# w_down by seven half-size products per quarter of the inner features, token-major

## Chip, core and metric

The kernel runs on one core of one Trainium2 chip. The metric is the device time of one execution in microseconds (us). A core has five engines that run their own instruction streams in order and wait for each other by semaphores: TensorE (PE; its weight loads are listed as PEld), VectorE (DVE), ScalarE (ACT), GpSimd (POOL) and SyncE (SP), which issues the DMAs here.

## Reference

One layer of a decoder on 512 tokens of width 1024: a token mixer (gated linear attention beside block-sparse attention), a squared-ReLU MLP, and a gated per-layer embedding, all in float32. The change lies in the MLP; what stands around it:

```python
y = jax.nn.sigmoid(gate_a) * y_a + jax.nn.sigmoid(gate_b) * y_b
x = x + y @ w_out[i]

h2 = rms_norm(x, norm_mlp[i])
x = x + jnp.square(jax.nn.relu(h2 @ w_up[i])) @ w_down[i]      # 1024 -> 4096 -> 1024

ple_gate = jax.nn.sigmoid(rms_norm(x, norm_ple[i]) @ w_ple_gate[i])
x = x + ple_gate * (p[i] @ w_ple[i])
```

## The kernel before

**Arithmetic.** Every large product is made of three matmuls (`mm3`, L99 to 103): both operands are split into a high half, rounded to the matmul's type, and a low half, the rest; high x high, high x low and low x high are added up in one PSUM bank. Splitting takes one ScalarE copy for the high half and one subtraction for the low half, on VectorE unless GpSimd is named (`split` L89, `halves` L150).

**Weights.** All weights come through one list, `stream` (L219 to 238), in units of 128 x 1024 elements (512 KB). `fetch` (L142) loads the next unit into one of three `raw` buffers by a DMA on SP's queue; `convert` (L168) pops the oldest raw, makes its high and low halves `whi` and `wlo` (three buffers each), puts the pair into `ready`, and fetches another. A unit's 24 matmuls use a pair from `ready`.

**Order of the work.** The schedule is by hand: program order is each engine's order. `gemm_fm` (L180) makes one 128-feature tile of a feature-major result (features in partitions, 512 tokens in columns): the weights are the stationary operand, and each unit is two halves of 12 matmuls, with a `tick` after each. `gemm_tm` (L196) makes a token-major result: activations are stationary and weights move. `tick` (L113) runs every job that is due for one step; jobs are generators started by `spawn` (L108), `yield 1` lets a job go on at the next tick, and `yield 0` later in the same tick. Small work of the other engines is so placed between halves of units. Results go to PSUM, two banks `acc` and six banks `aux`, and an evacuation (`evac`) reads them.

**The MLP (L747 to 790).** For each of two halves of the 4096 inner features: 16 tiles of w_up, each evacuated by VectorE (`up_evac` L754: ReLU and the norm's factor R1), squared by ScalarE (L765) and split into `ff` high and low; then 8 tiles of w_down with two units each (`nu=2`), added by VectorE to the residual stream `x1` (`down_evac` L769). x1 is feature-major and lies in SBUF slots c0 and c1. After the second half each tile is also scaled and split for the next product (`scaled_split` L94), its square is added up (`add_square` L303), and after the last tile `norm_end` (L293) is started: it splits the sum of squares at one tick, makes its mean over features on TensorE at the next (`mean_sq` L275), and then R2.

**The end.** `gemm_ple` (L795) makes four tiles of w_ple in 24 matmuls, `gemm_fm` eight tiles of w_gate, and the rest of w_ple follows.

Of the kernel before, what the change touches and what calls it, by code (L numbers as in the profile page):

```python
# [27 lines left out]
P = 128  # L28
# [18 lines left out]
def kernel(ctx: ExitStack, tc: tile.TileContext, xT, pT, w_in, w_val, w_glr, w2, cols,  # L47
# [5 lines left out]
    tmp = ctx.enter_context(tc.tile_pool(name="tmp", bufs=2))  # L53
    accp = ctx.enter_context(tc.tile_pool(name="acc", bufs=2, space=PSUM))
    auxp = ctx.enter_context(tc.tile_pool(name="aux", bufs=6, space=PSUM))
    ctx.enter_context(tc.manual_schedule())

    uid = [0]
# [49 lines left out]
    def spawn(gen, wait=0):  # L108


        jobs.append([gen, wait])

    def tick():  # L113
        due = []
        for j in list(jobs):
            if j[1] > 0:
                j[1] -= 1
            else:
                due.append(j)
        while due:  # L120
            again = []
            for j in due:
                try:
                    n = next(j[0])
                except StopIteration:
                    jobs.remove(j)
                    continue
                if n:
                    j[1] = n - 1
                else:  # L130
                    again.append(j)
            due = again
# [84 lines left out]
    def kt_of(hi, lo):  # L217
        return lambda k: (hi[:, k], lo[:, k])
# [514 lines left out]
    h2_lo = slot("a5", [P, KT, T], F32R)  # L733
    R1 = const.tile([P, T], F32, tag="R", name="R1")
    s1 = tt("s")

    def out_evac(i, ps):
# [9 lines left out]
    h3_hi = h3_lo = s2 = R2 = None  # L747
    for half in range(2):
        ff = [slot(t, [P, KT, T], F32R) for t in ("a0", "a1", "a2", "a6")]

        def ff_of(k, ff=ff):
            return ff[2 * (k // 8)][:, k % 8], ff[2 * (k // 8) + 1][:, k % 8]

        def up_evac(i, ps, half=half, ff_of=ff_of):  # L754
            e = tt("e")
            if half or i:
                V.scalar_tensor_tensor(e, ps, 0.0, R1, ALU.max, ALU.mult)  # L757
            else:
                A.activation(e, ps, AF.Relu)

            def rest():
                if not half and not i:
                    yield 2
                    V.tensor_tensor(e, e, R1, ALU.mult)
                A.activation(e, e, AF.Square)  # L765
                split(*ff_of(i), e)
            spawn(rest())

        def down_evac(i, ps, half=half):  # L769
            nonlocal h3_hi, h3_lo, s2, R2  # L770
            V.tensor_tensor(x1[i], ps, x1[i], ALU.add)  # L771
            if not half:
                return
            if i == 0:
                h3_hi = slot("a4", [P, KT, T], F32R)
                h3_lo = slot("a5", [P, KT, T], F32R)
                R2 = const.tile([P, T], F32, tag="R", name="R2")
                s2 = tt("s")
            scaled_split(h3_hi[:, i], h3_lo[:, i], x1[i], col[:, C_PLE + i:C_PLE + i + 1])
            add_square(s2, x1[i], i)  # L780
            if i == KT - 1:
                spawn(norm_end(R2, s2))

        gemm_fm(16, kt_of(h2_hi, h2_lo), up_evac)
        gemm_fm(8, ff_of, down_evac, nu=2)
        if not half:
            p_raw = slot("c2", [P, 2, T])
            p_hl = slot("c3", [P, 4, T], F32R)
            nc.sync.dma_start(out=p_raw, in_=pT)
            spawn(once(lambda: split(p_hl[:, :2], p_hl[:, 2:], p_raw)), 12)  # L790


    mid = slot("a0", [P, KT, T])

    def gemm_ple(evac, n=4):  # L795
        w = ready.pop(0)
        for i in range(n):
# [4 lines left out]
            if i == 3:  # L802
                convert()
            if i % 2:
                tick()
            evac(i, ps)
        return w

    def finish(i, e):
        V.tensor_tensor(e, e, x1[i], ALU.add)  # L810
        nc.sync.dma_start(out=outT[i * P:(i + 1) * P], in_=e)

    def ple0(i, ps):
# [1 line left out]

    def ple_gate(i, ps):
        e = tt("e") if i < 4 else mid[:, i]
        V.tensor_tensor(e, ps, R2, ALU.mult)
        A.activation(e, e, AF.Sigmoid)

        def rest():
            V.tensor_tensor(e, e, mid[:, i], ALU.mult)
            finish(i, e)
        if i < 4:
            spawn(once(rest))

    def ple1(i, ps):
        e = mid[:, 4 + i]
# [3 lines left out]
    def ple_last(w):  # L832

        for c in range(2):
# [8 lines left out]
            V.tensor_tensor(e, e, x1[KT - 1][:, s], ALU.add)  # L843
            nc.sync.dma_start(out=outT[(KT - 1) * P:, s], in_=e)

    gemm_ple(ple0)
    gemm_fm(8, kt_of(h3_hi, h3_lo), ple_gate)
    ple_last(gemm_ple(ple1, 3))


# [62 lines left out]
```

## Time and profile before

| | us |
|---|---|
| time, median of 3 runs | 975.72 (975.49 to 975.9) |
| profiled execution, its own time | 975.58 |
| its span, first to last instruction | 973.8 |
| TensorE matmul busy | 966.3 (99%), 4424 matmuls |
| VectorE / ScalarE / GpSimd busy | 522.1 (54%) / 431.7 (44%) / 105.9 (11%) |

How to read it: the span is split into busy time of each engine. The chain that ended last is followed back from the last instruction to what released it, step by step, and tells which engine set the time. A matmul's own duration (0.39 us) overlaps its neighbours; the distance between starts is its pace. The groups of instructions give the mean duration of each kind, and the timeline gives single instructions with their start.

### The profile page before, as it was taken

What the parts mean: (1) busy time and instruction counts of PE and PEld (TensorE: products, weight loads), DVE (VectorE), ACT (ScalarE), POOL (GpSimd) and SP (SyncE); (2) the same over time, 40 slices, a digit from 0 to 9 for tenths busy, and PEclk for the clock granted to TensorE, in tenths of its full rate; (3) what the DMA queues carried; (4) which work ended last, traced back from release to release, by engine and by line L of the source; (5) the groups of instructions that cost most, each with busy time, mean ns of one, the idle gap of its engine ahead of it and who ended that gap; (6) DMA issues with size and microseconds to landing.
All of it is one profiled execution on the core that took longest, in us unless ns stands there. A gap on an engine that the chain in (4) does not pass through costs nothing.

```text
span 973.8 us, 11302 instructions
## 1 busy us (share of the span) xinstructions
PE 966.3 (99%) x4424; PEld 804.1 (83%) x4424; DVE 522.1 (54%) x734; ACT 431.7 (44%) x657; POOL 105.9 (11%) x93
## 2 busy tenths in 40 slices
PE   9999999999999999999999999999999999999998
PEld 7888888878888888888888888888888888888886
DVE  5469889785556763333365555452233544344364
ACT  5558878774155743212323354442122443322531
POOL 0027675510321000000000000000000000000000
PEclk9999999999999999999999999999999999999999
DMA  7222121213211132343223223323323322323231
GB/s 259 87 87 82 48 78 45 72 60 108 87 65 44 68 127 87 108 140 140 88 90 105 89 84 109 108 87 108 98 98 108 102 93 94 101 93 102 86 130 44
DMA packets 26981, 92.83 MB, mean 95 GB/s; under 512 B 3120, under 2 KB 3504, under 8 KB 26672
## 3 DMA queue, kind: packets, MB, share of 16 engines
q1 hardware_dynamic: 26784, 92.09, 28.3%
q8 instruction: 35, 0.57, 0.2%
q14 instruction: 18, 0.15, 0.0%
q10 hardware_dynamic: 144, 0.02, 0.0%
HBM read 90.00 MB, written 2.10 MB: 95 GB/s over the span
## 4 chain that ended last, share of the span: by engine, by line
PE 97%; DVE 1%; ACT 1%; issue 0%; POOL 0%; POOLq 0%
PE acc L101 29%; PE acc L102 28%; PE acc L103 28%; PE aux L102 2%; PE aux L103 2%; PE aux L101 2%; PE aux L476 1%; PE aux L643 1%; PE aux L278 1%; PE aux L646 1%; PE aux L279 1%; PE aux L630 1%; PE aux L252 0%; PE aux L611 0%; DVE a L829 0%; PE acc L521 0%
## 5 line engine op out<-in xcount | busy, mean ns | idle before, releaser
L101 PE MATMUL acc<-a,whi 128*128 128x512 f32 x1088 | 425.5, 391 | 0.0
L102 PE MATMUL acc<-a,whi 128*128 128x512 f32 x1088 | 423.7, 389 | 0.0
L103 PE MATMUL acc<-a,wlo 128*128 128x512 f32 x1088 | 423.5, 389 | 0.0
L153 DVE TENSOR_TENSOR wlo<-raw,whi 128x1024 fp32r<-128x1024 f32 x160 | 203.5, 1272 | 112.8 <-ACT whi L151 110.8
L103 PEld LDWEIGHTS acc<-a,wlo 128*128 128x128 f32 x1088 | 204.2, 188 | 42.9
L101 PEld LDWEIGHTS acc<-a,whi 128*128 128x128 f32 x1088 | 204.3, 188 | 42.2
L102 PEld LDWEIGHTS acc<-a,whi 128*128 128x128 f32 x1088 | 204.3, 188 | 41.9
L151 ACT ACTIVATE whi<-raw 128x1024 fp32r<-128x1024 f32 x160 | 167.8, 1049 | 130.8 <-PE acc L102 109.1
L765 ACT ACTIVATE e<-e 128x512 f32<-128x512 f32 x32 | 20.2, 632 | 96.2 <-DVE e L757 92.9
L92 DVE TENSOR_TENSOR a<-e,a 128x512 fp32r<-128x512 f32 x40 | 27.7, 692 | 47.2 <-ACT a L91 47.2
L96 ACT ACTIVATE a<-c,col 128x512 fp32r<-128x512 f32 x16 | 11.6, 723 | 68.2 <-DVE c L771 42.3
L757 DVE SCALAR_TENSOR_TENSOR e<-acc,R 128x512 f32<-128x512 f32 x31 | 21.4, 690 | 34.6 <-PE acc L103 34.6
L91 ACT ACTIVATE a<-e 128x512 fp32r<-128x512 f32 x40 | 25.3, 632 | 32.6 <-DVE e L726 31.6
L771 DVE TENSOR_TENSOR c<-acc,c 128x512 f32<-128x512 f32 x16 | 11.1, 692 | 53.2 <-PE acc L103 53.2
L703 ACT ACTIVATE a<-a 128x512 f32<-128x512 f32 x16 | 10.1, 632 | 61.5 <-DVE a L702 61.5
L101 PE MATMUL acc<-c,whi 128*128 128x512 f32 (+1 forms) x82 | 31.8, 388 | 0.1
L406 POOL TENSOR_TENSOR ql<-q,qh 128x512 fp32r<-128x512 f32 x16 | 22.4, 1399 | 86.9 <-ACT qh L404 86.9
L102 PE MATMUL acc<-c,whi 128*128 128x512 f32 (+1 forms) x82 | 31.5, 384 | 0.0
L103 PE MATMUL acc<-c,wlo 128*128 128x512 f32 (+1 forms) x82 | 31.5, 384 | 0.0
L289 DVE SCALAR_TENSOR_TENSOR w<-aux,w 128x512 f32<-128x512 f32 x23 | 15.9, 691 | 28.5 <-ACT w L287 28.4
L450 POOL TENSOR_SCALAR c<-c,sm 128x512 f32<-128x512 f32 (+3 forms) x32 | 26.5, 839 | 18.9 <-DVE sm L449 18.9
L285 ACT ACTIVATE y<-aux,epsc 128x512 f32<-128x512 f32 x23 | 15.8, 685 | 26.8 <-PE aux L279 26.6
(176 smaller groups left out, 1024.1 us busy)
## 6 DMA issues: line engine op xcount, KB each, us to landing
raw<-in_w_in_dram SPq DMA_DIRECT2D x48, 512.0 KB, 3.3
raw<-in_w_up_dram SPq DMA_DIRECT2D x32, 512.0 KB, 3.3
raw<-in_w_down_dram SPq DMA_DIRECT2D x32, 512.0 KB, 3.3
raw<-in_w_val_dram SPq DMA_DIRECT2D x14, 512.0 KB, 3.3
raw<-in_w_a_dram SPq DMA_DIRECT2D x8, 512.0 KB, 3.3
raw<-in_w_b_dram SPq DMA_DIRECT2D x8, 512.0 KB, 3.2
raw<-in_w_out_dram SPq DMA_DIRECT2D x8, 512.0 KB, 3.3
raw<-in_w_gate_dram SPq DMA_DIRECT2D x8, 512.0 KB, 3.4
```

Of the source, the lines that this page charges most:

```text
L91: A.activation(hi, src, AF.Copy)
L92: (eng or V).tensor_tensor(lo, src, f32(hi), ALU.subtract)
L101: PE.matmul(ps, a[0], b[0], start=start, stop=False)
L102: PE.matmul(ps, a[0], b[1], start=False, stop=False)
L103: PE.matmul(ps, a[1], b[0], start=False, stop=stop)
L151: A.activation(hi, src, AF.Copy)
L153: (eng or V).tensor_tensor(lo, src, f32(hi), ALU.subtract)
L289: V.scalar_tensor_tensor(w, ps, EPS, w, ALU.add, ALU.mult)
L406: G.tensor_tensor(sl, q2, f32(sh), ALU.subtract)
L450: G.tensor_scalar(t, t, sm, 1.0, ALU.mult, ALU.mult)
L757: V.scalar_tensor_tensor(e, ps, 0.0, R1, ALU.max, ALU.mult)
L765: A.activation(e, e, AF.Square)
```

## The change

w_down's product is made by Strassen's scheme in Winograd's form. The 4096 inner features are taken in four quarters of 1024. In each, the activations (512 tokens x 1024) are cut into 2 x 2 blocks of 256 tokens x 512 features, and w_down's part (1024 x 1024) into 2 x 2 blocks of 512 x 512. Seven products of sums of blocks replace eight products of blocks. The activations are the stationary operand, so the result `acc` is token-major, and `turn_back` turns it by TensorE's transposes, adds the residual, and goes on to the norm.

The work of the other engines: GpSimd makes the sums of weight blocks (`add` in `down_units`) and most differences of activations (`rest` in `ahead_of`; the last tile's are VectorE's); each sum is split into halves like any weight (`make`); each left operand is split into `ta` or `tb` (`t_split`); each product's two banks are added into `acc` by VectorE (`subtotal`), some through `y` by GpSimd. Weights are no longer taken from the stream by `convert`: every load and every split is put at a fixed tick (`at`; `unit` loads seven ticks and splits three ticks ahead of use). T0 = 178 is the tick of w_up's first half unit. In the first three quarters four tiles of the next quarter's w_up stand behind products 4, 5, 6 and 7; the last quarter has none. x1's slots are needed for weight blocks, so x1 is written to DRAM (`spill`) and read back as `x2`. w_down is laid out by rows (`_rows`) on the host.

The diff, cut to its core:

```diff
+    plan = {}
+    ticks = [0]
+    def at(t, f):
+        plan.setdefault(t, []).append(f)
     def tick():
+        for f in plan.pop(ticks[0], []):
+            f()
+        ticks[0] += 1
         due = []
...
-    for half in range(2):
-        stream += [w_up[16 * half + j, 0] for j in range(16)]
-        stream += [w_down[j, 2 * half + u] for j in range(8) for u in range(2)]
-    stream += [w_ple[0]] + [w_gate[j, 0] for j in range(8)] + [w_ple[1]]
+    T0 = 178
+    def unit(c, src):
...
+        at(c - 7, load)
+        at(c - 3, lambda: make(box[0]))
+    def make(raw):
+        hi = wp.tile([P] + list(raw.shape[1:]), F32R, tag="whi", name=nm("whi"))
+        lo = wp.tile([P] + list(raw.shape[1:]), F32R, tag="wlo", name=nm("wlo"))
+        ready.append((hi, lo))
+        jobs.insert(0, [halves(hi, lo, raw), 0])
+    def down_units(g):
+        d0 = T0 + 30 * g + 16
+        gap = 2 if g < 3 else 0
...
+        def add(out, a, b):
+            G.tensor_tensor(out(), a(), b(), ALU.add)
+        for u in range(2):
...
+            at(d0 + u - 8, load(u, "A21", "c0", a21))
+            at(d0 + u - 8, load(u, "A22", "c3", a22))
+            at(d0 + u - 5, load(u, "A11", "c1", a11))
+            at(d0 + u - 5, lambda S=S, W=W: add(S, W("A21"), W("A22")))
+            at(d0 + u - 3, lambda S=S: make(S()))
+            at(d0 + u - 1, lambda S=S, W=W: add(S, S, W("A11")))
+            at(d0 + u - 1, lambda W=W: make(W("A11")()))
+            at(d0 + u - 1, load(u, "A12", "c3", a12))
+            at(d0 + u + 1, lambda S=S: make(S()))
+            at(d0 + u + 2, lambda W=W: add(W("A21"), W("A21"), W("A11")))
+            at(d0 + u + 3, lambda W=W: make(W("A12")()))
+            at(d0 + u + 4, load(u, "A22b", "c1", a22))
+            at(d0 + u + 4, lambda S=S, W=W: add(S, S, W("A12")))
+            at(d0 + u + gap + 5, lambda W=W: make(W("A21")()))
+            at(d0 + u + 2 * gap + 7, lambda S=S: make(S()))
+            at(d0 + u + 3 * gap + 9, lambda W=W: make(W("A22b")()))
...
+        nc.sync.dma_start(out=spill[:, i], in_=x1[i])
...
+        def up_evac(i, ps):
+            e = F[:, :, i]
...
+            def rest():
...
+                A.activation(e, e, AF.Square)
+                yield 1
+                k = i % 4
+                if i < 4:
...
+                    G.tensor_tensor(box[0][:, k], F[:, 0, i], F[:, 1, i], ALU.subtract)
+                else:
+                    eng = V if i == 7 else G
+                    d = F[:, 1, k]
+                    eng.tensor_tensor(d, d, F[:, 1, i], ALU.subtract)
+                    eng.tensor_tensor(F[:, 0, k], F[:, 0, k], d, ALU.subtract)
...
+        later(d0 - 6, t_split(ta, 1, F[:, 0, :4]))
+        at(d0 - 5, lambda: spawn(t_split(ta, 0, box[0])))
+        later(d0 + 2, t_split(tb, 0, F[:, 0, :4]))
+        later(d0 + 3, t_split(tb, 1, F[:, 0, 4:]))
+        later(d0 + 4, t_split(ta, 0, F[:, 1, :4]))
+        at(d0 + 4, lambda: G.tensor_tensor(F[:, 0, 4:], F[:, 0, 4:], F[:, 0, :4], ALU.subtract))
+        later(d0 + 6, t_split(ta, 1, F[:, 1, 4:]))
+        later(d0 + 8, t_split(tb, 0, F[:, 0, 4:]))
+        gemm_fm(8 if g == 0 else 4, kt_of(h2_hi, h2_lo), lambda i, ps: up_evac(i + (4 if g else 0), ps))
...
+        for m, ps in enumerate(product(ta, 0)):
+            subtotal(new, part(0, 1, m), ps, ALU.add)
+            subtotal(new, part(1, 1, m), ps, ALU.subtract)
...
+        for m, ps in enumerate(product(ta, 1)):
+            A.activation(y[m], ps, AF.Copy)
+            subtotal(new, part(0, 0, m), ps, ALU.add)
+        tick()
+        for m, ps in enumerate(product(tb, 0)):
+            V.tensor_tensor(y[m], ps, y[m], ALU.subtract)
+            G.tensor_tensor(part(0, 1, m), part(0, 1, m), y[m], ALU.subtract)
+        tick()
+        for m, ps in enumerate(product(tb, 1)):
+            subtotal(False, part(0, 0, m), ps, ALU.add)
+        tick()
+        up_ahead(0)
...
+        if g == 3:
+            at(d0 + 12, lambda: turn_back(0))
+            at(d0 + 13, lambda: turn_back(2))
...
+    def turn_back(i0):
...
+        for i in range(i0, i0 + 2):
+            ps = bank()
+            for m in range(NT):
+                PE.transpose(ps[:, m * P:(m + 1) * P], acc[:, m, i * P:(i + 1) * P], ident)
...
+            V.tensor_tensor(x2[:, i], ps, x2[:, i], ALU.add)
+            scaled_split(h3[0][:, i], h3[1][:, i], x2[:, i], col[:, C_PLE + i:C_PLE + i + 1])
...
+                A.activation(q, x2[:, i], AF.Square)
+                G.tensor_tensor(s2, s2, q, ALU.add)
             if i == KT - 1:
                 spawn(norm_end(R2, s2))
...
             if i % 2:
+                if back:
+                    turn_back(back.pop(0))
                 tick()
```

## Rows read from the trace of the kernel before

**Rows 1.** The page: busy us and share, granted clock by slices, chain by engine.
```profile
PE 966.3 (99%) x4424; PEld 804.1 (83%) x4424; DVE 522.1 (54%) x734; ACT 431.7 (44%) x657; POOL 105.9 (11%) x93
...
PEclk9999999999999999999999999999999999999999
...
PE 97%; DVE 1%; ACT 1%; issue 0%; POOL 0%; POOLq 0%
```
**Rows 2.** TensorE's waits, longest first: line, releaser: us, times, longest.
```profile
PE aux L252 <- DVE ones L248: 2.2, 1, 2.2
```
**Rows 3.** Timeline of TensorE in w_up: start, duration (us), line, operation.
```profile
590.20 0.39 PE L101 MATMUL acc<-a,whi 128*128 128x512 f32 x1
...
590.88 0.39 PE L101 MATMUL acc<-a,whi 128*128 128x512 f32 x1
```
**Rows 4.** Timeline of TensorE in a token-major product.
```profile
225.50 0.39 PE L101 MATMUL acc<-whi,a 128*128 128x512 f32 x1
...
226.18 0.39 PE L101 MATMUL aux<-whi,a 128*128 128x512 f32 x1
```
**Rows 5.** Busy by stretches: length, then PE, PEld, DVE, ACT, POOL, clock, DMA.
```profile
60.00:230.00 170.00, 168.94 (x836) 142.12 (x835) 142.80 (x272) 134.94 (x267) 85.66 (x71) 1.00 0.21 68
...
570.00:655.00 85.00, 85.00 (x376) 70.37 (x375) 42.23 (x50) 39.51 (x54) 0.00 (x0) 1.00 0.29 99
```
**Rows 6.** Timeline of TensorE around eight transposes of the attention stage.
```profile
93.26 1.03 PE L476 MATMUL aux<-ident,c 128*128 128x128 f32 x8
94.05 0.48 PE L101 MATMUL aux<-c 128*128 128x512 f32 x1
94.36 0.40 PE L102 MATMUL aux<-c 128*128 128x512 f32 x1
```
**Rows 7.** Groups of instructions by form: count, busy us, mean ns of one.
```profile
L153 DVE TENSOR_TENSOR wlo<-raw,whi 128x1024 fp32r<-128x1024 f32 x160 | 203.5, 1272 | 112.8 <-ACT whi L151 110.8
L151 ACT ACTIVATE whi<-raw 128x1024 fp32r<-128x1024 f32 x160 | 167.8, 1049 | 130.8 <-PE acc L102 109.1 <-issue 19.3 <-DMA raw<-in_w_val_dram 2.3
...
L765 ACT ACTIVATE e<-e 128x512 f32<-128x512 f32 x32 | 20.2, 632 | 96.2 <-DVE e L757 92.9 <-DVE e L764 3.3
...
L96 ACT ACTIVATE a<-c,col 128x512 fp32r<-128x512 f32 x16 | 11.6, 723 | 68.2 <-DVE c L771 42.3 <-DVE c L738 25.9
...
L771 DVE TENSOR_TENSOR c<-acc,c 128x512 f32<-128x512 f32 x16 | 11.1, 692 | 53.2 <-PE acc L103 53.2
```
**Rows 8.** Instructions of a line: duration in ns, min/median/max, first and last start.
```profile
L153 DVE TENSOR_TENSOR wlo<-raw,whi x160: 1204/1225/2309, 14.4 to 955.3; 128x1024 fp32r<-128x1024 f32 x160
L153 POOL TENSOR_TENSOR c<-y,c x16: 1289/1301/2281, 68.2 to 187.0; 128x512 fp32r<-128x512 f32 x16
...
L843 DVE TENSOR_TENSOR a<-a,c x2: 424/424/424, 969.8 to 970.5; 128x256 f32<-128x256 f32 x2
```
**Rows 9.** The page: DMA issues, KB each, median us to landing.
```profile
raw<-in_w_down_dram SPq DMA_DIRECT2D x32, 512.0 KB, 3.3
```
**Rows 10.** Timelines of GpSimd and VectorE around 242 us.
```profile
242.18 1.72 POOL L597 TENSOR_TENSOR c<-c,e 128x512 f32<-128x512 f32 x1 [38.55 <-ACT whi L151]
...
242.07 0.69 DVE L596 TENSOR_TENSOR c<-c,e 128x512 f32<-128x512 f32 x1
242.68 2.31 DVE L153 TENSOR_TENSOR wlo<-raw,whi 128x1024 fp32r<-128x1024 f32 x1
```
**Rows 11.** Timelines of GpSimd and VectorE around 122 us.
```profile
121.49 1.31 POOL L153 TENSOR_TENSOR c<-y,c 128x512 fp32r<-128x512 f32 x1
...
122.25 0.69 DVE L289 SCALAR_TENSOR_TENSOR w<-aux,w 128x512 f32<-128x512 f32 x1 [0.53 <-ACT w L287]
```
**Rows 12.** Timeline of VectorE, a low half and what is queued behind it.
```profile
125.42 1.21 DVE L153 TENSOR_TENSOR wlo<-raw,whi 128x1024 fp32r<-128x1024 f32 x1
126.56 0.68 DVE L153 TENSOR_TENSOR a<-aux,a 128x512 fp32r<-128x512 f32 x1
```
**Rows 13.** Timelines of VectorE and TensorE at the norm R2.
```profile
914.08 0.69 DVE L771 TENSOR_TENSOR c<-acc,c 128x512 f32<-128x512 f32 x1 [3.30 <-PE acc L103]
...
919.62 0.40 PE L278 MATMUL aux<-qh,ones 128*128 128x512 f32 x1
```

More of the change, by code (lines that the diff above doesn't have):

```diff
@@ L55 @@
     auxp = ctx.enter_context(tc.tile_pool(name="aux", bufs=6, space=PSUM))
+    dram = ctx.enter_context(tc.tile_pool(name="dram", bufs=1, space=bass.MemoryType.DRAM))
     ctx.enter_context(tc.manual_schedule())
@@ new lines, in make, with load, f, W @@
+    def make(raw):
[6 more added lines that the diff above has]
+        gap = 2 if g < 3 else 0
+        box = {}
+        def load(t, name, tag, src):
+            def f():
+                if name not in box:
+                    box[name] = [slot(f"{tag[0]}{int(tag[1:]) + j}", [P, 2, 512]) for j in range(2)] \
+                        if tag[0] == "v" else slot(tag, [P, 2, 2, 512])
+                nc.sync.dma_start(out=box[name][:, t % 2], in_=src)
+            return f
+        def add(out, a, b):
+            G.tensor_tensor(out(), a(), b(), ALU.add)
+        for u in range(2):
+            a11, a12 = w_down[0, 4 * g + u], w_down[0, 4 * g + 2 + u]
+            a21, a22 = w_down[1, 4 * g + u], w_down[1, 4 * g + 2 + u]
+            def W(name, u=u):
+                return lambda: box[name][:, u]
+            def S(u=u):
+                if u not in sums:
+                    sums[u] = slot(f"v{u}", [P, 2, 512])
+                return sums[u]
+            at(d0 + u - 8, load(u, "A21", "c0", a21))
[14 more added lines that the diff above has]
+            at(d0 + u + 3 * gap + 9, lambda W=W: make(W("A22b")()))
@@ L241 @@
+    sums = {}
+    for g in range(4):
+        for j in range(8):
+            c = T0 + 30 * g + 2 * j
+            unit(c if g == 0 or j > 3 else c - 6 + 2 * j, w_up[8 * g + j, 0])
+        at(T0 + 30 * g + 8, sums.clear)
+        down_units(g)
+    TP = T0 + 120
+    unit(TP, w_ple[0])
+    for j in range(8):
+        unit(TP + 2 + 2 * j, w_gate[j, 0])
+    unit(TP + 18, w_ple[1])
     ident = const.tile([P, P], F32, name="ident")
@@ L735 @@
     s1 = tt("s")
+    spill = dram.tile([P, KT, T], F32, name="spill")
     def out_evac(i, ps):
@@ L744 @@
     gemm_fm(8, kt_of(y_hi, y_lo), out_evac)
[L747 to L757, printed above, removed]
+    acc = None
+    h3 = []
@@ new lines, with subtotal, half_of, ahead_of @@
+    s2 = R2 = x2 = p_hl = None
+    def subtotal(first, out, ps, op):
+        if not first:
+            V.tensor_tensor(out, out, ps, op)
+        elif op == ALU.add:
+            A.activation(out, ps, AF.Copy)
+        else:
+            V.tensor_scalar(out, ps, -1.0, None, ALU.mult)
+    def half_of(t):
+        return t.rearrange("p (t c) -> p t c", t=2)
+    ffs = {}
+    def ahead_of(g):
+        F = slot("a0", [P, 2, KT, 256])
+        box = []
+        def up_evac(i, ps):
+            e = F[:, :, i]
+            if g or i:
+                V.scalar_tensor_tensor(e, half_of(ps), 0.0, half_of(R1), ALU.max, ALU.mult)
@@ L758, in up_evac @@
             else:
-                A.activation(e, ps, AF.Relu)
+                A.activation(e, half_of(ps), AF.Relu)
             def rest():
-                if not half and not i:
+                if not g and not i:
                     yield 2
-                    V.tensor_tensor(e, e, R1, ALU.mult)
+                    V.tensor_tensor(e, e, half_of(R1), ALU.mult)
                 A.activation(e, e, AF.Square)
-                split(*ff_of(i), e)
-            spawn(rest())
[L769 to L776, printed above, removed]
+                yield 1
@@ L785, with back_x1, load_p @@
[L785 to L793, printed above, removed]
+    def back_x1():
+        nonlocal x2
+        x2 = slot("a4", [P, KT, T])
+        nc.sync.dma_start(out=x2, in_=spill)
+    def load_p():
+        nonlocal p_hl
+        raw = wp.tile([P, 2, T], F32, tag="raw", name=nm("raw"))
+        nc.sync.dma_start(out=raw, in_=pT)
+        yield 6
+        p_hl = slot("c0", [P, 4, T], F32R)
+        yield from halves(p_hl[:, :2], p_hl[:, 2:], raw)
@@ L795, in gemm_ple @@
+    at(T0 + 106 + 1, back_x1)
+    at(T0 + 106 + 3, lambda: spawn(load_p()))
+    for g in range(4):
+        up_down(g)
+    mid = slot("a1", [P, KT, T])
+    back = [4, 6]
     def gemm_ple(evac, n=4):
@@ L900 @@
         "w_up": _columns(a["w_up"][0]),
-        "w_down": _columns(a["w_down"][0]),
+        "w_down": _rows(a["w_down"][0]),
         "w_gate": _columns(a["w_ple_gate"][0]),
```

93 lines of the change are left out of this document (84 added, 9 removed).

## Prediction

> **What bounds the kernel now.** I read the shares and the chain first: TensorE is busy for 99% of the span, the chain that ended last is 97% TensorE, and the granted clock is full in every slice [rows 1]. Then its waits: the longest of all is 2.2 us, at the start [rows 2]. So TensorE is never late for anything, and the time is the number of its matmuls times their pace. Two matmuls of one stream start 0.68 us apart with two between them, 0.227 us each [rows 3]; a half unit of 12 is 2.72 us, and one of these passes between two ticks. The token-major order, which the change takes, has the same pace: 0.68 us from 225.50 to 226.18 [rows 4]. Last the stages: in the 85 us of w_up from 570, VectorE is busy for 42.2 us, ScalarE for 39.5 us and GpSimd not at all; only in the attention stage does GpSimd work much, 85.7 of 170 us, beside 142.8 us of VectorE [rows 5]. Every cover the change uses is in these idle parts.
>
> **What is removed.** w_down has 32 units of 24 matmuls, 768. Seven half-size products of 24 for each of four quarters are 672. 96 matmuls go: 96 x 0.227 = 21.8 us.
>
> **What TensorE gets.** The result is token-major and is turned back by 32 transposes, eight at a time (`turn_back`). Eight transposes in the trace take from 93.26 to 94.05, 0.79 us, and behind the first matmul after them the next comes in 0.31 instead of 0.23 us [rows 6]. That is 0.87 us for eight, 3.5 us for 32, all on TensorE's path, since its stream has no gap to put them in. Net on TensorE: 21.8 - 3.5 = 18.3 us less. With nothing late the profiled 975.6 us (973.8 span and 1.8 around it; 0.1 us from the median of the runs) would become 957.3 us.
>
> **What the other engines get.** Per quarter, and a quarter is 30 half units or 81.6 us of TensorE:
> - VectorE makes the low half of 14 units of w_down instead of 8, 1.22 us each in the median, and ScalarE the high half, 1.05 us [rows 7, 8]. Seven left operands of 1024 columns are split at the same prices. It makes 16 additions out of PSUM in place of 4, 0.69 us each [rows 7].
> - GpSimd makes the sums of weight blocks, 8 of 1024 columns; the differences of the activations, 10 of 256 and one of 1024; and 6 of 512. One of 512 takes 1.30 us when undisturbed [rows 8]. No row has the others. VectorE goes from 0.69 us to 1.22 us for twice the columns and to 0.42 us for half [rows 7, 8], and by these ratios GpSimd takes 2.3 us and 0.8 us (bounds 1.3 to 2.6 and 0.65 to 1.3). Sum about 37 us.
> - DMA: 10 loads of 512 KB instead of 8, 3.3 us each from issue to landing [rows 9], and x1 out to DRAM and back. They are issued four or more ticks ahead (10.9 us), so I cost them at nothing; without that cover one late load costs at most its 3.3 us.
>
> Neither sum fills 81.6 us. But these engines aren't independent. At 242 us VectorE runs an addition of two SBUF tensors; GpSimd's, queued at 242.18, takes 1.72 us in place of 1.30, and VectorE's next, a low half queued at 242.68, takes 2.31 us in place of 1.22: GpSimd, which asked before VectorE's second, was let in when VectorE's first was over (at 242.76), was through at 243.90, and VectorE's second ended 1.1 us after that [rows 10]. So operations with two SBUF inputs on VectorE and operations on GpSimd exclude each other, first come first served. One input from PSUM escapes: VectorE's 0.69 us from 122.25 overlap the end of GpSimd's 1.31 us from 121.49, and neither is longer for it [rows 11]. The Trainium skill's page "SBUF — State Buffer", section "Who interferes with whom", says this as a rule: a VectorE instruction with two SBUF inputs contends with a GpSimd one that reads SBUF, and the later one blocks fully; the trace agrees.
>
> So I count one **lock**. Per quarter it has VectorE's 22 low halves of weights and 7 of operands (29 x 1.22 = 35 us) and GpSimd's 37 us: 72 of 81.6 us. On average this still fits. It doesn't where the work is bunched, and that is around the third product.
>
> **The third product.** Let t = 0 be where TensorE begins the first product of a quarter; product 3 begins 4 half units later, at 10.9, and its third matmul, which reads the low half of its left operand (`tb`, slot 0), at 11.3. What must pass the lock first? w_up's fifth tile of the quarter leaves TensorE at -16.3. Its evacuation (0.69), its square (0.63) and the split of product 2's operand, which reads what it is about to overwrite (1.05 + 1.22), end at about -12.5, and the low half of a weight unit (1.15, the distance at which queued ones follow each other [rows 12]) holds the lock until -11.4. From there on the lock has work without a break, in the order of the queues: on GpSimd three pairs of 256-column differences (4.8), `S` of the second half-block, `S += A11` twice, `A21 += A11` twice and the first `S += A12` (6 x 2.3 = 13.8); on VectorE the low halves of product 1's operand, of six weight units and of `tb` (8 x 1.15 = 9.2) and the two differences of w_up's last tile (0.8). Sum 28.6, so `tb` is split at 17.2: TensorE waits 5.9 us. If `S += A12` comes in behind and not between the two differences, 3.6 us. GpSimd at 2.6 us per sum would make it 7.7 us. I take 4.7 us, the middle of the first two, four times: 18.8 us.
>
> This wait is also there in small without any lock: behind the end of product 1 (5.6) VectorE has four PSUM additions, two low halves of weights, the two differences and the low half of `tb` in its queue, 4 x 0.61 + 3 x 1.15 + 0.8 = 6.7 us, until 12.3, 1.0 us late.
>
> **Later in a quarter.** Behind product 3 the lock still owes the difference of 1024, two of `y`, the last `S += A12` and three low halves. The w_up tile after product 4 and the fifth product find their low halves about 0.5 and 0.8 us late by the same count, in the three quarters with w_up tiles in between: 1.3 x 3 = 3.9 us (bounds 0 and 6).
>
> **The last quarter** has no such tiles. From the end of that wait to the second half of product 7 TensorE has 26.7 us of work, the lock 13 low halves (the split of p among them) and 12.4 us of GpSimd, 27 us, and VectorE 6 us of PSUM additions in the same queue; `turn_back` puts transposes between the two halves of product 7 that wait for product 6's additions. I take 6 us (bounds 2 and 10).
>
> **The tail.** The norm R2 needs all of x2. Before, from the last matmul of w_down to the mean's matmul there are 24 matmuls of w_ple, and the last addition at 914.08 is 5.5 us ahead of the mean at 919.62 [rows 13]; nothing waits. After, `norm_end` starts at the last `turn_back` and the mean's matmuls stand one half unit, 2.7 us, behind it. Behind the transposes: the addition for tile 6 and its high half (0.69 + 0.72), the addition for tile 7, high half and square (0.69 + 0.72 + 0.63 [rows 7]), GpSimd's addition (1.3), and split (0.6 + 0.7) give 6 to 7 us. TensorE waits 4 us (bounds 0, if another wait covers it, and 4.5).
>
> **Sum:** 975.6 - 18.3 + 18.8 + 3.9 + 6 + 4 = 990.0 us. With all low bounds (14.4, 0, 2, 0) 973.7 us; with the high ones (23.6, 6, 10, 4.5) 1001.4 us.
>
> **Rivals.**
> - *The lock is hidden.* If the queues are further ahead than I laid out (sums of weights need only DMAs and earlier readers), only VectorE's own 1 us in each quarter, and some 3 us at the end, are left: 957.3 + 7 = 964 us, 957 to 973. For it: average lock load 88%, and idle VectorE before each quarter. Against it: GpSimd's first differences wait for TensorE, and the whole chain stands behind them in one queue. It turns to my forecast as soon as the lock is more than about 4 us behind at product 3.
> - *The clock falls* in the waits. The trace shows no wait above 2.2 us and full clock [rows 1, 2], so nothing in it speaks of a longer one. If TensorE's clock goes from 2.4 to 1.2 GHz in each of five waits and the half unit behind it runs at half pace, that is up to 2.7 us more each, 13 us: about 1000 us, to 1010. The Trainium skill's page "TensorE: Matmul & The Clock Gate", section "HAM oscillation — how this bites in real kernels", says that idle gaps between bursts of matmuls bring the clock down to the lower level; the run of the kernel before has no such gap.
> - *DMA is late.* SP's queue is in order, and a load whose buffer isn't free holds up those behind it; at a mean load of 0.29 [rows 5] that seems harmless. One or two 3.3 us waits per quarter on TensorE would give 957 + 7 + 13 to 26: 977 to 990 us.
>
> **How the numbers follow.** Forecast (974 to 1001) 0.57; hidden lock 0.29; clock 0.10; DMA 0.04. What the measurement can tell from no change is about 0.2%, 2 us: 973.8 to 977.7. Slower: 0.52 of the forecast, 0.10 and 0.03 of the DMA case, 0.65; same: 0.04 + 0.01 = 0.05; faster: 0.29 and 0.01 of the forecast's low end, 0.30. The range takes in the forecast and the slower half of the hidden lock (964 and up, about 0.15), the DMA case and half of the fallen clock (0.06): 964 to 1003, 0.82. The forecast's own range is 974 to 1001.
>
> **What would show it.** TensorE's waits should name VectorE's split of `a` (slot `a2`) at the first matmuls of product 3 of each quarter, 3 to 7 us each. GpSimd's 1024-column sums and VectorE's 1024-column low halves should be lengthened by each other there, a low half up to 3.5 us. R2's mean should wait some 4 us for its split. TensorE should have 96 matmuls fewer and 32 transposes more. I am wrong if TensorE has no wait above 2 us in product 3, or if the sums on GpSimd run far ahead.

## The result, and the profile after

The changed kernel takes 1000.31 us (998.76 to 1002.3) where the kernel before takes 975.81 us (975.49 to 975.99): a ratio of 1.0253 [1.0234, 1.0271]. The profiled execution took 999.96 us with a span of 998.2 us, against 975.6 and 973.8 us. The forecast was 990.0 us, slower, for the reason that product 3 of each quarter waits; that wait is there, and 10 us more than the forecast.

The page of the changed kernel, which answers to [rows 1]:

```profile
PE 965.1 (97%) x4360; PEld 799.5 (80%) x4360; DVE 634.9 (64%) x807; ACT 471.0 (47%) x691; POOL 302.9 (30%) x200
...
PEclk9999999999999999999999999999899989989799
```

64 instructions fewer (96 matmuls out, 32 transposes in), and yet nearly the same busy time: some of them ran longer. The row of the clock says where: the granted clock is below 9 tenths in four slices of 25 us near the end; three hold the product 3 of a quarter (at 707, 796 and 884 us), the fourth the end of w_down and w_ple. TensorE's waits, which answer to [rows 2] (line, releaser: us in total, times, longest):

```profile
PE aux L104 <- DVE a L164: 14.9, 4, 3.7
PE acc L102 <- ACT a L1052: 6.3, 2, 3.7
PE aux L338 <- DVE ones L334: 2.2, 1, 2.2
PE aux L991 <- DVE a L850: 2.2, 2, 1.9
PE aux L364 <- ACT qh L92: 2.0, 1, 2.0
```

The third is that of [rows 2], in both kernels. The first is product 3, once in each quarter, for the low half (L164) of its left operand. The second, at tiles of w_ple for ScalarE's copy of the tile before (L1052), nobody had announced. The fourth is the first `turn_back` in the last quarter, for product 6's additions; the last is R2's mean. Between the starts of matmuls in the timeline these are distances of 4.07, 4.13, 4.12 and 4.13 us at product 3, and with the normal 0.227 us off each, 15.6 us; the others come to 2.6 + 4.1 (w_ple), 2.2 and 2.2. That is 26.7 us.

The rest is pace. Stretches of the third quarter, in the columns of [rows 5], with product 3 waiting in the first, its matmuls in the second, and what follows in the third:

```profile
795.00:800.00 5.00, 1.27 (x6) 0.55 (x4) 5.00 (x4) 3.28 (x5) 3.26 (x1) 0.88 0.98 381
800.00:806.00 6.00, 6.00 (x15) 4.72 (x16) 3.65 (x5) 1.39 (x2) 2.38 (x1) 0.53 0.04 15
806.00:840.00 34.00, 34.00 (x152) 28.13 (x151) 26.37 (x23) 13.12 (x14) 16.33 (x9) 1.00 0.14 47
```

A granted clock of 0.53 is nearly the lower of its two levels (1.2 of 2.4 GHz), already as the wait ends, and full again 6 us later. In TensorE's timeline (start, duration, line, operation):

```profile
795.81 0.39 PE L103 MATMUL aux<-wlo,a 128*128 128x512 f32 x1
799.94 0.79 PE L104 MATMUL aux<-whi,a 128*128 128x512 f32 x1 [3.73 <-DVE a L164]
800.53 0.63 PE L102 MATMUL aux<-whi,a 128*128 128x512 f32 x1
800.96 0.63 PE L103 MATMUL aux<-wlo,a 128*128 128x512 f32 x1
...
805.63 0.39 PE L102 MATMUL aux<-whi,a 128*128 128x512 f32 x1
```

From 799.94 to 805.63 stand 13 matmuls, 5.69 us in place of 13 x 0.227 = 2.95 us: 2.7 us more behind a wait of 3.9 us. Added up over all starts, matmuls at 0.4 us and more instead of 0.227 cost about 13.3 us, some 9 behind the four product 3's and the rest in the last quarter and the tail.

So the last matmul starts 24.5 us later (993.87 instead of 969.41): 18.3 us saved as worked out, 26.7 us of waits, 13.3 us of half pace, in all 21.7 us more. Of the 2.8 us that are left, some 1.2 are single matmuls at 0.25 to 0.38 us, and 0.8 the last eight transposes, which took 1.56 us at the lower clock (938.86 to 940.42) in place of 0.79; the rest isn't traced.

Why product 3 waits is in the other two engines. VectorE (its low half for product 3 is the last line), then GpSimd:

```profile
788.64 2.49 DVE L164 TENSOR_TENSOR wlo<-c,whi 128x1024 fp32r<-128x1024 f32 x1 [0.25 <-ACT whi L162]
791.06 2.47 DVE L850 TENSOR_TENSOR a<-a,aux 128x512 f32<-128x512 f32 x4
...
794.24 2.35 DVE L164 TENSOR_TENSOR wlo<-v,whi 128x1024 fp32r<-128x1024 f32 x2
796.51 3.38 DVE L164 TENSOR_TENSOR a<-a,a 128x1024 fp32r<-128x1024 f32 x1
```
```profile
786.66 6.75 POOL L282 TENSOR_TENSOR c<-c,c 128x1024 f32<-128x1024 f32 x2
795.54 3.26 POOL L282 TENSOR_TENSOR v<-v,c 128x1024 f32<-128x1024 f32 x1 [2.13 <-DVE wlo L164]
803.50 2.38 POOL L915 TENSOR_TENSOR a<-a 128x1024 f32<-128x1024 f32 x1 [4.70 <-DVE a L164]
```

This is [rows 10] at twice the size. GpSimd's `S += A12` is set free by VectorE's low half of a weight, asks at 795.54 while VectorE runs the next one (until 796.6), gets in, and holds until 798.8; `tb`'s low half, queued at 796.51, takes 3.38 us in place of 1.22 and ends 1.1 us after GpSimd. GpSimd's `A21 += A11` at 786.66 had held VectorE's weight from 788.64 in the same way.

### The profile page after: what moved, and what is told of

The parts are those of the page before. It is cut to its first block, busy times and chain, and to the rows that moved or that the text cites. A ratio compares the mean times of both kernels' runs of the same rounds, so it can differ in the third digit from the quotient of the medians.

```text
span 998.2 us, 11425 instructions
## 1 busy us (share of the span) xinstructions
PE 965.1 (97%) x4360; PEld 799.5 (80%) x4360; DVE 634.9 (64%) x807; ACT 471.0 (47%) x691; POOL 302.9 (30%) x200
## 4 chain that ended last, share of the span: by engine, by line
PE 88%; DVE 8%; ACT 2%; issue 1%; POOLq 0%; POOL 0%; ACTq 0%; DVEq 0%
PE acc L102 22%; PE acc L103 22%; PE acc L104 22%; PE aux L104 6%; PE aux L103 6%; PE aux L102 6%; DVE wlo L164 3%; DVE a L164 2%; DVE a L850 1%; PE aux L562 1%; ACT whi L162 1%; PE aux L729 1%; PE aux L365 1%; PE aux L364 1%; PE aux L732 1%
## 5 line engine op out<-in xcount | busy, mean ns | idle before, releaser
L102 PE MATMUL acc<-a,whi 128*128 128x512 f32 x832 | 326.4, 392 | 0.0
L103 PE MATMUL acc<-a,whi 128*128 128x512 f32 x832 | 324.3, 390 | 0.0
L104 PE MATMUL acc<-a,wlo 128*128 128x512 f32 x832 | 324.1, 390 | 0.0
L164 DVE TENSOR_TENSOR wlo<-raw,whi 128x1024 fp32r<-128x1024 f32 x128 | 167.7, 1313 | 79.3 <-ACT whi L162 77.9
L104 PEld LDWEIGHTS acc<-a,wlo 128*128 128x128 f32 x832 | 156.3, 188 | 32.9
L102 PEld LDWEIGHTS acc<-a,whi 128*128 128x128 f32 x832 | 156.6, 188 | 32.2
L103 PEld LDWEIGHTS acc<-a,whi 128*128 128x128 f32 x832 | 156.5, 188 | 31.8
L104 PE MATMUL aux<-whi,a 128*128 128x512 f32 x288 | 116.9, 406 | 14.9 <-DVE a L164 14.9
L102 PE MATMUL aux<-whi,a 128*128 128x512 f32 x288 | 116.8, 406 | 0.0
L103 PE MATMUL aux<-wlo,a 128*128 128x512 f32 x288 | 115.9, 402 | 0.0
L104 PEld LDWEIGHTS aux<-whi,a 128*128 128x128 f32 x288 | 56.6, 197 | 28.6 <-DVE a L164 16.6
L164 DVE TENSOR_TENSOR wlo<-c,whi 128x1024 fp32r<-128x1024 f32 x32 | 53.0, 1672 | 22.9 <-ACT whi L162 22.9
L102 PEld LDWEIGHTS aux<-whi,a 128*128 128x128 f32 x288 | 56.7, 197 | 12.7 <-ACT a L162 0.8
L103 PEld LDWEIGHTS aux<-wlo,a 128*128 128x128 f32 x288 | 56.7, 197 | 12.5 <-DVE wlo L164 0.4
L282 POOL TENSOR_TENSOR v<-v,c 128x1024 f32<-128x1024 f32 x16 | 45.8, 2861 | 8.3 <-DVE wlo L164 8.3
L164 DVE TENSOR_TENSOR a<-a,a 128x1024 fp32r<-128x1024 f32 x24 | 43.3, 1804 | 6.6 <-ACT a L162 6.6
L164 DVE TENSOR_TENSOR wlo<-v,whi 128x1024 fp32r<-128x1024 f32 x24 | 41.2, 1742 | 7.6 <-ACT whi L162 7.6
```

The lines of the kernel that those rows point to most:

```text
L102: PE.matmul(ps, a[0], b[0], start=start, stop=False)
L103: PE.matmul(ps, a[0], b[1], start=False, stop=False)
L104: PE.matmul(ps, a[1], b[0], start=False, stop=stop)
L164: (eng or V).tensor_tensor(lo, src, f32(hi), ALU.subtract)
L282: G.tensor_tensor(out(), a(), b(), ALU.add)
```

## The experiments

All ratios are against the kernel before, run beside each.

**Without the sums of weights.** GpSimd's eight sums per quarter left out:

```diff
 def add(out, a, b):
-    G.tensor_tensor(out(), a(), b(), ALU.add)
+    return
...
-    at(d0 + u - 3, lambda S=S: make(S()))
+    at(d0 + u - 3, lambda W=W: make(W("A21")()))
```

> The changed kernel without GpSimd's sums of weight blocks: the eight additions of 1024 columns per quarter are left out, and the blocks themselves are split in their place (this part of the product is left out, the other work stays). Theory (GpSimd and VectorE exclude each other): TensorE's wait at product 3 falls from 3.7 us to 1 us or less in each quarter, the granted clock doesn't fall there, VectorE's low halves of weights go from 1.7 us in the mean to 1.2 to 1.3, and the time falls by 4 x 2.7 to 3.7 us of waits and some 9 us of half pace, to 975 to 981 us; the tail's waits stay. Rival (VectorE's own queue is too long at product 3, with no part of GpSimd's in it): the wait stays at 3 to 4 us and the time at 997 to 1002 us. Rival (operands wait for GpSimd's results): as the theory; the next run parts them.

980.09 us, 1.0046 [1.0031, 1.0061]. Its waits:

```profile
PE acc L102 <- ACT a L1052: 7.1, 2, 4.1
...
PE aux L104 <- DVE a L164: 1.8, 4, 0.4
```

Product 3 waits 0.4 instead of 3.7 us, and no half pace follows it. So the sums on GpSimd cause that wait; what is left, VectorE's own queue and GpSimd's differences, gives at most 0.4 us. VectorE's low halves of w_down's weights take 1.52 us in the mean, not the expected 1.2 to 1.3; GpSimd's differences and its additions of `y` are still there. The 980 us also say that without any sum the change is still slower, for the most part by its tail: w_ple's tiles alone wait 7.1 us.

**As many additions on GpSimd, with nobody waiting.** In place of each sum, a spare tile is added to itself (the splits are those of the run without sums):

```diff
-    G.tensor_tensor(out(), a(), b(), ALU.add)
+    G.tensor_tensor(dummy[i], dummy[i], dummy[i], ALU.add)
```

> As the run without sums, but at the same places in GpSimd's queue stands an addition of the same size of a spare tile to itself, on which nothing waits (the sums of blocks are left out as before). Theory (exclusion): the low halves are held up as in the changed kernel, the wait at product 3 is 2.5 to 4 us, and the time 990 to 1002 us. Rival (operands wait for GpSimd's results): nothing waits for these additions, the wait at product 3 is 1 us or less, and the time 975 to 981 us as in the run without sums.

984.45 us, 1.0086 [1.007, 1.0103]; between the two expectations. Product 3's wait, GpSimd's timeline, and the line of VectorE that answers to 796.51 above:

```profile
PE aux L104 <- DVE a L164: 5.4, 4, 1.5
```
```profile
771.10 1.89 POOL L287 TENSOR_TENSOR v<-v 128x1024 f32<-128x1024 f32 x1
...
775.44 9.42 POOL L287 TENSOR_TENSOR v<-v 128x1024 f32<-128x1024 f32 x4
793.24 2.40 POOL L921 TENSOR_TENSOR a<-a 128x1024 f32<-128x1024 f32 x1 [8.39 <-DVE a L164]
```
```profile
788.48 1.22 DVE L164 TENSOR_TENSOR a<-a,a 128x1024 fp32r<-128x1024 f32 x1
```

Waiting for no data, the dummies ran ahead, four on end, and none stood beside `tb`'s low half. So exclusion by additions that nobody waits for costs 1.1 us more than no sums at all (1.5 against 0.4). Sums would cost more: a tile added to itself takes 1.89 us undisturbed, a sum 2.40, so the load here is lighter. That the other 2.2 us come from where the data's releases put the last sum, exactly ahead of `tb`, isn't shown here; the run with one sum moved tests it.

**The sums behind product 3.** `A21 += A11` and `S += A12`, four of the eight sums, issued behind the difference of 1024, and the load of `A22b` a tick later:

```diff
-    at(d0 + u + 2, lambda W=W: add(W("A21"), W("A21"), W("A11")))
+    late.setdefault(g, []).append(lambda W=W: add(W("A21"), W("A21"), W("A11")))
...
-    at(d0 + u + 4, load(u, "A22b", "c1", a22))
-    at(d0 + u + 4, lambda S=S, W=W: add(S, S, W("A12")))
+    at(d0 + u + 5, load(u, "A22b", "c1", a22))
+    at(d0 + u + 5, lambda S=S, W=W: add(S, S, W("A12")))
...
+    for f in late[g]:
+        at(d0 + 4, f)
```

> The whole computation. In GpSimd's queue A21 += A11 and S += A12 (products 5 and 6 need them) stand behind the 1024-column difference, which itself waits for the split of product 4's operand; so four sums of 2.4 us go from before product 3 to behind it. Theory (exclusion): 7 us of work leave VectorE's way ahead of product 3; the wait there falls to 0 to 1.3 us, the clock stays up in the first three quarters, and the time falls to 976 to 986 us; in the last quarter, where no w_up tiles stand between, products 5 and 6 get 0 to 3 us of waits instead. Rival (VectorE's own queue): the wait at product 3 stays at 3 to 4 us, 997 to 1002 us. Rival (the sum of the two engines' work sets the pace wherever it lies): the waits move to products 5 and 6 of each quarter at 3 us each, 995 to 1002 us.

1000.16 us, 1.0258 [1.0242, 1.0273]: nothing gained, as the third of the expectations had it. Product 3 waits at most 0.5 us, and two new waits stand on TensorE's list; below them GpSimd's timeline:

```profile
PE acc L104 <- DVE wlo L164: 8.5, 4, 2.9
...
PE aux L103 <- DVE wlo L164: 4.9, 5, 2.7
```
```profile
800.58 2.40 POOL L915 TENSOR_TENSOR a<-a 128x1024 f32<-128x1024 f32 x1 [13.38 <-DVE a L164]
802.94 6.70 POOL L282 TENSOR_TENSOR c<-c,c 128x1024 f32<-128x1024 f32 x2
```

GpSimd idles for 13.38 us, until product 3 is under way, and pays behind it; the low halves of the weights for the next tiles are late instead. The backlog only moved.

**Keeping TensorE busy in the wait.** 16 matmuls on constants ahead of each product 3, 64 in all, whose result is unused:

```diff
+    for _ in range(16):
+        PE.matmul(pre, ones[P], ones[P].rearrange("p (o c) -> p o c", o=1).to_broadcast([P, NT, P]),
+                  start=True, stop=True)
     for m, ps in enumerate(product(tb, 0)):
```

> The changed kernel with 16 matmuls of constants more before product 3 of each quarter (3.6 us at full pace, into a bank that nobody reads): TensorE works where it waited. Theory (the fall of the clock costs 2 to 2.6 us behind each wait, beside the wait): the wait at product 3 is under 0.5 us, the granted clock stays full there, and the time falls by 6 to 9 us to 991 to 995 us although 64 matmuls are added. Rival (the matmuls behind the wait are slow for another reason, VectorE's or GpSimd's traffic): they stay at 0.43 us apart, and the time stays at 998 to 1002 us.

995.51 us, 1.0206 [1.019, 1.0221]: 4.8 us less than the changed kernel, with 64 matmuls more, and half a us short of the expected gain. The stretch that had a clock of 0.53 and 15 matmuls, and the timeline ahead of it:

```profile
800.00:806.00 6.00, 6.00 (x28) 4.99 (x27) 5.72 (x5) 4.53 (x5) 2.41 (x1) 1.00 0.00 0
```
```profile
792.04 3.84 PE L958 MATMUL aux<-ones 128*128 128x512 f32 x16
...
797.14 0.50 PE L104 MATMUL aux<-whi,a 128*128 128x512 f32 x1 [0.79 <-DVE a L164]
797.48 0.40 PE L102 MATMUL aux<-whi,a 128*128 128x512 f32 x1
```

The same lock, the same traffic, a full clock, and matmuls 0.23 us apart from the second one behind the wait. So the half pace is the clock's and follows TensorE's idleness; it isn't contention for operands. The gain is smaller than the 9 us of half pace: the fill and what remains of the waits take as long as the waits did, and a weight that is late in the last quarter costs a new 2.2 us and half pace behind it.

**The tail.** w_ple's copies ahead of `turn_back`, both additions of a pair ahead of its splits, and R2's mean three half units behind:

```diff
-    spawn(norm_end(R2, s2))
+    spawn(norm_end(R2, s2, 3))
...
+    evac(i, ps)
     if i % 2:
         if back:
             turn_back(back.pop(0))
         tick()
-    evac(i, ps)
```

> The changed kernel with the end in another order: w_ple's tiles are copied out of PSUM by ScalarE ahead of the work of turn_back and not behind it, turn_back makes both additions to x2 before the first split (VectorE then doesn't wait for ScalarE between them), and R2's mean stands three half units behind its split instead of one. Theory (the waits behind product 7 are these three queues): the waits of 2.6, 4.1 and 2.2 us there go to under 1 us together, and with them some 4 us of half pace; 1000.3 falls to 986 to 990 us, and the four waits at product 3 stay at 3.7 us. Rival (VectorE is late there because of the exclusion in the last quarter, whatever the order): the waits stay, 996 to 1002 us.

992.31 us, 1.0172 [1.0157, 1.0187], 8 us less than the changed kernel and 2 more than expected. w_ple's waits go from 6.3 to 2.0 us and the mean's is gone, but a late weight takes 1.7 us in their place:

```profile
PE acc L102 <- ACT a L1053: 2.0, 2, 1.2
PE acc L104 <- DVE wlo L164: 1.7, 1, 1.7
```

The two waits as they stood in the changed kernel, and ScalarE ahead of the second:

```profile
930.57 0.50 PE L102 MATMUL acc<-c,whi 128*128 128x512 f32 x1 [2.59 <-ACT a L1052]
...
936.13 0.79 PE L102 MATMUL acc<-c,whi 128*128 128x512 f32 x1 [3.68 <-ACT a L1052]
```
```profile
934.36 0.72 ACT L97 ACTIVATE a<-a,col 128x512 fp32r<-128x512 f32 x1 [0.90 <-DVE a L997]
935.50 1.06 ACT L1052 ACTIVATE a<-acc 128x512 f32<-128x512 f32 x2
```

ScalarE's copies of w_ple's tiles are queued behind the high halves and squares of `turn_back`, which wait for VectorE's additions; until a copy has run, its PSUM bank isn't free. The wait is for ScalarE's queue order, not for its work.

**One sum moved.** `S += A12` a tick later. In GpSimd's queue this changes the first half-block's place alone: it falls behind the difference of 1024 and two of `y`, where the second's stood already:

```diff
-    at(d0 + u + 4, lambda S=S, W=W: add(S, S, W("A12")))
+    at(d0 + u + 5, lambda S=S, W=W: add(S, S, W("A12")))
```

> The changed kernel with only S += A12 of the first half-block moved in GpSimd's queue, behind the 1024-column difference and the two additions of y. In the changed kernel this sum is set free by the low half of product 3's first weight and is in VectorE's way just before the split of product 3's operand, which it makes 2.2 us longer. Theory (exclusion): the wait at product 3 falls by these 2.2 us to 1.3 to 1.7 us, the clock stays up there, nothing comes up at product 5 in the first three quarters, 980 to 987 us. Rival (as in the run with four sums moved, the backlog only moves): waits of together 3 us or more in each quarter and half pace behind them, 995 to 1001 us.

990.21 us, 1.0149 [1.0134, 1.0165]. Product 3's wait, `tb`'s low half on VectorE, and the two sums on GpSimd:

```profile
PE aux L104 <- DVE a L164: 6.2, 4, 1.6
```
```profile
791.26 1.22 DVE L164 TENSOR_TENSOR a<-a,a 128x1024 fp32r<-128x1024 f32 x1
```
```profile
804.87 6.71 POOL L282 TENSOR_TENSOR v<-v,c 128x1024 f32<-128x1024 f32 x2
```

The low half takes its 1.22 us again, the wait at product 3 goes from 3.7 to 1.6 us, and no matmul behind it is at half pace; 10 us for one tick. It missed the expected 980 to 987 us by 3: the last quarter, without tiles of w_up to hide behind, got a new wait of 2.8 us for a weight, and R2's mean waits 3.1 instead of 2.0 us.

**Both.** The last two edits together:

> Both edits, of the end and of S += A12. If the causes are separate, the gains add up: 1000.3 less 11 to 14 and less 14 to 20 us, 967 to 975 us, faster than the kernel before (975.3). If they share a cause (one backlog in the last quarter), less is left of the second: 976 to 985 us.

981.51 us, 1.0058 [1.0041, 1.0075]. The time lies where I expected it for a backlog that the last quarter and the tail share; but the gains add up (8.0 and 10.1 us alone, 18.8 together), so the run doesn't show that they share one. What is left on TensorE's list:

```profile
PE aux L104 <- DVE a L164: 6.3, 4, 1.6
PE aux L103 <- DVE wlo L164: 4.1, 5, 2.8
```

**Earlier sums.** On top of the last, the first sum of each half-block and its two loads two ticks earlier (`d0 + u - 7` for `- 5`, `- 10` for `- 8`):

> As the one before, and the first sums, S = A21 + A22, and their loads two ticks earlier, so that they stand ahead of the differences of w_up's fifth tile in GpSimd's queue, in a stretch where GpSimd idles. Theory (at product 3 the lock is behind because of all that is queued on it from t = -11 on): one sum of 2.4 us leaves that stretch, the wait at product 3 goes from about 1.5 to under 0.5 us, 3 to 6 us less than the run before. Rival (the wait that is left is VectorE's own queue, 1.0 us): no more than 1 us less per quarter and at most 2 us in all.

981.15 us, 1.005 [1.0035, 1.0065], no difference from the one before, as the rival had it. Product 3's waits come to 5.1 us in four instead of 6.3: most of the wait isn't that of a queue which begins too late, and what was gained there went into other waits (0.8 us for ScalarE's split of an operand, in the first quarter).

**VectorE relieved ahead of product 3.** On top of both edits, two of product 1's four PSUM additions put behind product 2:

```diff
-    subtotal(new, part(1, 1, m), ps, ALU.subtract)
...
+    for m, ps in enumerate(first):
+        subtotal(new, part(1, 1, m), ps, ALU.subtract)
```

> As the run with both edits (981.5 us), and two of product 1's four additions out of PSUM stand behind product 2 instead of ahead of product 3's splits in VectorE's queue (1.2 us less there, outside the lock). If the 1.6 us that are left at product 3 are VectorE's own queue, as the run with the earlier first sum suggests, the wait falls to 0.3 to 0.6 us in each quarter and the time by 3.5 to 6 us, to 975.5 to 978 us. Rival (they are the lock's): 0 to 1 us less in all, 980.5 to 981.5 us.

980.50 us, 1.005 [1.0036, 1.0063], and product 3 still waits 1.5 us: my expectation fell. VectorE was there earlier and had to wait; VectorE, then GpSimd:

```profile
785.53 1.27 DVE L850 TENSOR_TENSOR a<-a,aux 128x512 f32<-128x512 f32 x2
786.72 1.43 DVE L887 TENSOR_TENSOR a<-a 128x256 f32<-128x256 f32 x1
```
```profile
781.13 6.73 POOL L282 TENSOR_TENSOR c<-c,c 128x1024 f32<-128x1024 f32 x2
```

The difference of 256 columns, 0.42 us alone, takes 1.43: GpSimd's second `A21 += A11` is in the way until 787.86. So 1.0 of the last 1.5 us is the lock's too.

**The last quarter in the plain product.** On top of that, the last quarter as eight half-size products in place of seven, token-major, without sums of weights, 24 matmuls more:

```diff
-    for g in range(4):
+    for g in range(3):
         up_down(g)
+    last_quarter()
```

> As the one before, and the last quarter of the inner features is multiplied in the plain way, token-major, by eight units of 24 matmuls instead of seven products (24 matmuls, 5.4 us, more), without sums on GpSimd and without differences; half of the turning back then lies beside it. Theory (the last quarter's waits come from the lock, because no w_up tiles stand between its products): its waits of 7 us and its half pace of 4 to 5 us go, and the time falls by 5 to 8 us net to 968 to 972 us, faster than the kernel before (975.5). Rival (they are the tail's, not the quarter's): the waits stay and the 5.4 us come on top, 980 us or more.

974.46 us (974.07 to 975.09), beside 975.76 us: 0.9987 [0.9978, 0.9996]. It misses the expected 968 to 972 us, and is the first version below the kernel before, by 1.3 us, a difference of 0.13%. Its page, and the largest waits of TensorE:

```profile
PE 957.3 (98%) x4384; PEld 794.0 (82%) x4384; DVE 618.0 (63%) x792; ACT 460.9 (47%) x684; POOL 263.9 (27%) x175
```
```profile
PE aux L104 <- DVE a L164: 4.6, 3, 1.5
PE acc L104 <- DVE wlo L164: 2.9, 3, 1.6
```

The clock is full. TensorE's work is 9.0 us less than before [rows 1], and most of that goes into these waits.

**The second `A21 += A11` behind.** On top of that, one of the sums in front of product 3 (the second of the two in the line at 781.13 above) put behind the difference of 1024, and the load of `A22b` a tick later:

> As the run with the plain last quarter (974.5 us), and of the two sums A21 += A11 the second stands behind the 1024-column difference in GpSimd's queue. With product 1's additions put off, VectorE's differences of w_up's last tile waited 1.0 us for this sum, and the wait at product 3 stayed at 1.5 us. Theory (exclusion, first come first served): the differences take 0.42 us instead of 1.43, the wait at product 3 falls to 0.4 to 0.7 us in each of three quarters, and the time to 970.5 to 973 us. Rival (the backlog only moves, as with four sums): the w_up tile or product 5 behind it waits 1 us longer, 974 to 976 us.

976.29 us (976.16 to 979.46), 1.0016 [1.0007, 1.0025], some 2 us worse. Product 3's waits fall to 1.5 us in three, at most 0.5, so the 1.0 us was the lock's; but the weights' rise:

```profile
PE acc L104 <- DVE wlo L164: 8.8, 5, 2.8
...
PE aux L104 <- DVE a L164: 1.5, 3, 0.5
```

What leaves the front of product 3 comes back behind it, as with four sums moved, and dearer.

## Why the prediction was right, and where it was off

**Right.** The direction, the place and the mechanism. TensorE's side came out as counted: 4360 instructions, and 18.3 us saved, a figure that isn't measured by itself but fits the time to 2.8 us. The wait at product 3 names VectorE's split of slot `a2` in each quarter; it was put at 3.6 to 5.9 us, taken as 4.7, and is 3.9. That it lies near the low bound is luck: there `S += A12` stays behind `tb`'s low half, and in the run it stands right ahead of it, as the high bound has it. What is shorter is the list of work for the lock, 28.6 us from -11.4 on (773.2 in the third quarter). In the timelines of both engines the lock is taken without a break from there until `tb`'s low half ends at 799.89, 26.7 us; most of the difference is the first of the three pairs of 256-column differences on GpSimd, which was through at 773.76:

```profile
772.17 1.59 POOL L888 TENSOR_TENSOR a<-a 128x256 f32<-128x256 f32 x1 [1.47 <-DVE a L164]
773.72 3.39 POOL L282 TENSOR_TENSOR v<-c,c 128x1024 f32<-128x1024 f32 x1
```

The sums themselves took 2.40 us undisturbed (the estimate was 2.3), the 256-column differences 0.74 (0.8), the lengthened low half 3.38 (up to 3.5). Leaving the sums out took that wait away, and moving the one that stood ahead of `tb` took 2.1 of its 3.7 us, so this cause is shown, not argued. VectorE's own queue was put at 1.0 us late and, with the sums left out, is 0.4 us late at most. I had one detail of VectorE's order wrong: the differences of w_up's last tile come before the low halves of `S`, which cost nothing.

**The mis-sized term: the clock.** It stood among the rivals, at a chance of 0.10 and up to 13 us, as if it were an alternative to the waits. It is their consequence: the same four waits that I had put into the sum at 4.7 us each took the clock down with them, and some 9 us came on top, 13.3 with those behind the waits of the last quarter and the tail. The rival's price was right, and its chance and its place were not. I had argued that the trace of before speaks of no long wait [rows 1, 2], which is true and no reason, since the forecast itself brought waits of that length in. It belonged into the sum: 990 and 13 would have been 1003. The Trainium skill's page "TensorE: Matmul & The Clock Gate", section "HAM oscillation — how this bites in real kernels", tells of a kernel in which a wait for DMA ahead of each burst of matmuls makes each burst start at the lower clock; the four product 3's agree, at 0.43 us a matmul for 8, 11, 13 and 13 matmuls.

**Later in a quarter** I had 3.9 us for late low halves behind product 3, and there are none in the first three quarters. The reason is visible in the timeline of GpSimd: it waits 4.70 us for the split of product 4's operand before its next operation at 803.50, and all of the quarter's sums but one are done by then, so little was owed. With four sums behind product 3 such waits appeared (8.5 and 4.9 us), and with one sum behind, in the version with the plain last quarter, 8.8 us. That the wait at product 3 itself gave the low halves their time, so that I had added two terms that exclude each other, is likely and not shown: in both runs sums had been moved there.

**The last quarter** was put at 6 us (2 to 10), and is 2.2: the additions ahead of the transposes, as described; the low halves were not late. **The tail** was put at 4 us, all at R2's mean. The mean waits 2.2, and w_ple's tiles 6.7: I had counted what `turn_back` adds to VectorE and ScalarE, and followed it to the mean only, not to the copies that stand behind it in ScalarE's queue and that set free a PSUM bank. With the copies in front (and the two other edits of the tail) that wait is 4.3 us shorter.

**In sum:** the waits were forecast at 18.8 + 3.9 + 6 + 4 = 32.7 us and are 26.7; the half pace, 13.3 us, was forecast at nothing. The measured time is in the range, at its upper end, and at the top of the forecast's own; it is there by some luck, since waits put 6 us too high made up for part of the half pace.

**Still open:** why no version ends more than 1.3 us below the kernel before, although TensorE has 9.0 us less to do in the best. The last two moves of sums came back as other waits; but whether VectorE and GpSimd simply have too much exclusive work around product 3, or whether an order exists that fits, wasn't settled.

## What to carry to other kernels

When a change puts a wait of some microseconds into a TensorE that had none, count the wait and the matmuls behind it at half pace in the same sum; here a wait of 3.9 us cost 6.6 in the third quarter. Add up what two engines do under one lock in the stretch in which it's due, not over the stage, and ask who sets free the operation that comes just ahead of the one on the path: putting one sum behind three other operations was worth 10 us here. And follow each new step to everything that is queued behind it on its engine, down to the copy which frees a PSUM bank.

## What the runs showed of the hardware

- After a single wait of 3.7 us TensorE's clock stood at 1.2 GHz when work came back (a granted clock of 0.88 in the stretch with the wait, 0.53 in the 6 us behind it), and 8 to 13 matmuls ran at 0.43 us before it rose. Behind the wait of 1.9 us at the first transposes five were slow; behind the waits of 1.5 to 1.6 us at product 3, in the runs with a sum moved, none.
- Useless work can be cheaper than an idle TensorE: 64 matmuls on constants in its waits made the kernel 4.8 us faster.
- GpSimd's addition of two 128x1024 f32 tiles takes 2.40 us, 3.39 when a VectorE operation with two SBUF inputs is in front of it; each of the two engines can be held up for most of the other's operation (VectorE's low half took 3.38 us in place of 1.22), and the one that asked first goes before what the other engine has queued later.
